# A hybrid decoder trunk in fp32: ScalarE of the mixer in written order, convolved tiles and gates finished in steps of slots, decay operands in other rooms

## The chip, the cores and the metric

The program runs on one NeuronCore of one Trainium2 chip, as one launch. The metric is the device time in microseconds (us). The kernel before took 2068.75, 2069.67 and 2070.12 us in three runs, so a median of 2069.67 us. Its profiled execution took 2069.44 us, of which 2067.7 us lie in the span of the profile. The names of the engines are TensorE (PE in the profile), VectorE (DVE), ScalarE (ACT), GpSimd (POOL) and SyncE (SP), which issues most of the transfers.

## The reference

Input and output are 512 positions of 1024 channels in fp32, and there are two layers. Cut to what matters here:

```python
# twice:
x = x + 0.5 * swiglu_1(rmsnorm(x))          # 1024 -> 2816 -> 1024
x = x + mixer(rmsnorm(x)) @ w_out
x = x + 0.5 * swiglu_2(rmsnorm(x))
# mixer: one projection of h, split into the inputs of three heads' groups
hg_q, hg_f, hg_i, hg_g, gd_q, gd_k, gd_v, gd_z, gd_b, gd_a, rg_x, rg_gate = split(h @ w_in)
# HGRN2, 4 heads of 64:   f = lb + (1-lb)*sigmoid(hg_f), k = 1-f, q = silu(hg_q)
#                         S_t = diag(f_t) S_{t-1} + k_t v_t^T,  o_t = S_t^T q_t
# gated delta, 4 of 128:  q, k, v = silu(conv4(...)), q and k normalised by head
#                         g = -exp(a_log)*softplus(gd_a + dt_bias), beta = sigmoid(gd_b)
#                         S_t = e^g_t (I - b_t k_t k_t^T) S_{t-1} + b_t k_t v_t^T
# RG-LRU, 256 channels:   xc = conv4(rg_x) + bias; r, i = sigmoid(block matmuls of xc)
#                         a = exp(-8 r softplus(-lam)); h_t = a_t h_{t-1} + sqrt(1-a_t^2) (i xc)_t
# each gated (silu(hg_g), silu(gd_z), gelu(rg_gate)), concatenated, projected by w_out
```

## The kernel before

Activations lie with channels on the 128 partitions and the 512 positions along the free axis. Every weight tile is split into two halves of fp32r: ScalarE casts it (`whi`, L229), VectorE forms the rest (`wlo`, L230). A product is then three matmuls: xh·whi (L268), xl·whi (L269) and xh·wlo (L270). One output tile of a projection (128 channels by 512 positions) is 8 steps of 3 matmuls. Its weights come as two tiles, of four steps each, and each tile needs one cast, one subtraction and one transfer.

The mixer of a layer issues 26 such projections in the order `MIX_ORDER` (k0 to k3 of the gated delta rule, then f and q of HGRN2, q0 to q3, v0 to v3, rx0, rx1, rg0, rg1, hg0, hg1, z0 to z3). `Slots.run` (L92) walks through them. One slot is two steps, 6 matmuls. After each slot every side line whose wait is over does its next piece; a line says with `yield (event, n)` that it wants n slots from an event, and with `yield n` that it wants n more slots. A projection's event is fired when its `then` (L575) has evicted the tile and issued the work behind it: the eviction by VectorE (times the row factor `rb`), for k, q, v and rx also the convolution (L588 or L590 on ScalarE and three L592 on VectorE), and silu, sigmoid or gelu on ScalarE.

In the mixer TensorE runs in the order in which the Python code issues its instructions: `manual_schedule(engines={PE})`, L610. The order of the other engines is set by a scheduler, which places their instructions by its own estimate of when each can start. All engines run their lists in order.

Three pieces of the mixer matter below. `gdn_gates` forms g (the `log1pexp` chain of small VectorE instructions, L501 to L519, L720) and from it eight tiles of 128 by 512 in fp32r (L730), the operands of eight decay matmuls (L747); ScalarE takes exp of three small matmuls (`gex`, L738) and of the decays (`DT`, L751). `gdn_k` transposes the silu'd keys (L760), sums their squares (L766), scales them (`Kn`, L795) and makes k·k (L786), whose result VectorE multiplies by DT (L787). `rglru` (the gate matmuls L1294, sigmoid L1296, Exp L1302, Tanh L1303, L1306 and L1307 on VectorE, Sqrt L1308, then L1310, the scan L1312 and L1313 on VectorE) stands beside the chunk chain of the gated delta rule (`chain`: L971, L979, L983, L995, L1007 on TensorE; L986, L989 and L1015 on ScalarE; L974, L1002 and L1011 on VectorE) and the HGRN2 products (`hgrn`: L1127, L1149, with copies L1140 and L1152 on ScalarE).

Of the kernel before, what the change touches and what calls it, by code (L numbers as in the profile page):

```python
# [6 lines left out]
F32R = mybir.dt.float32r  # L7
I32 = mybir.dt.int32
AF = mybir.ActivationFunctionType
# [4 lines left out]
P = 128  # L14
L = 2
D = 1024
S = 512
# [14 lines left out]
C_RCW = C_CW + 48  # L32
# [29 lines left out]
class Slots:  # L62
# [11 lines left out]
        event, n = w  # L74
        return event in self.at and self.now >= self.at[event] + n

    def add(self, line):
        self.sides.append([(None, 0), line])
        self.at.setdefault(None, 0)

    def step(self):

# [31 lines left out]
class Trunk:  # L114
# [452 lines left out]
    def project(self, then, event=None):  # L567

        ps = self.bank()
        w = self.weights()  # L570
        for k in range(KT):
            self.mm3_step(ps, w, self.X, k, KT, k)
            if k % 2 and k < KT - 1:
                yield
        then(ps)  # L575
        if event is not None:
            self.sl.fire(event)
        yield

    def conv(self, ps, w, bias=None):  # L580

        nc = self.nc
        pad = self.tmp((P, S + 4))
        nc.gpsimd.memset(pad[:, 0:4], 0.0)
        nc.vector.tensor_tensor(pad[:, 4:], ps, self.rb, ALU.mult)
        c = self.tmp()
        if bias is None:
            nc.scalar.activation(c, pad[:, 4:], AF.Copy, scale=w[3])  # L588
        else:
            nc.scalar.activation(c, pad[:, 4:], AF.Identity, scale=w[3], bias=bias)  # L590
        for i in range(3):
            nc.vector.scalar_tensor_tensor(c, pad[:, 1 + i:1 + i + S], w[i], c, ALU.mult, ALU.add)  # L592
        return c
# [13 lines left out]

    def mixer(self, l, nxt):
        nc = self.nc
        with self.tc.manual_schedule(engines={mybir.EngineType.PE}):  # L610
            self.mixer_in(l)
            self.mixer_out(l, nxt)

# [71 lines left out]
    def in_gd(self, l, m):  # L685

        c0 = l * NPC + C_CW + 4 * m

        def then(ps):
            if m == 0:  # L690
                self.Q = self.tile(self.mp, (P, 4, S), F32, "r_q")
            if m == 4:
                self.kt = self.spare(3)
            if m < 4:
                out = self.Q[:, m, :]
            elif m < 8:
                out = self.kt[:, m - 4, :]
            else:
                out = self.vt[m] = self.tmp()
            c = self.conv(ps, [self.par[:, c0 + i:c0 + i + 1] for i in range(4)])  # L700
            self.silu(out, c)

        self.vt = getattr(self, "vt", {})
        return self.project(then, f"gd{m}")

    def gdn_gates(self, l, ba):

        nc = self.nc
        sl = self.sl
        c0 = l * NPC  # L710
        v3 = lambda t: t.rearrange("p (c h) -> p c h", h=4)
        self.beta = self.tile(self.mp, (P, 16), F32, "beta")
        y = self.small(16, "g_y")
        dt = self.par[:, c0 + C_DT:c0 + C_DT + 4][:, None, :].to_broadcast([P, NJ, 4])
        nc.vector.tensor_tensor(v3(y), ba[:, :, 4:8], dt, ALU.add)
        sp = self.small(16, "g_sp")
        self.log1pexp(sp, y, 16)
        self.g = self.tile(self.mp, (P, 16), F32, "g")
        nea = self.nea[:, 4 * l:4 * l + 4][:, None, :].to_broadcast([P, NJ, 4])
        nc.vector.tensor_tensor(v3(self.g), v3(sp), nea, ALU.mult)  # L720
        gh = [self.small(16, f"g_{t}", F32R) for t in "hl"]
        nc.vector.tensor_copy(gh[0], self.g)
        nc.vector.tensor_tensor(gh[1], self.g, gh[0].bitcast(F32), ALU.subtract)

        low = self.tile(self.mp, (P, 4, S), F32R, "r_q")
        gm = []
        for c in range(NJ):
            gm.append([self.tile(self.mp, (P, 4, P), F32R, "gt", 4).rearrange("p a b -> p (a b)"), low[:, c, :]])
            for t, o in zip(gh, gm[c]):
                nc.vector.tensor_tensor(o.rearrange("p (a b) -> p a b", b=P),  # L730
                                        self.le[:, None, :].to_broadcast([P, 4, P]),
                                        bc(t[:, 4 * c:4 * c + 4].bitcast(F32), P), ALU.mult)
        yield 12
        ps = self.bank("mx", (P, 3, 16))
        for i, lhs in enumerate((self.le, self.gt, self.one)):
            nc.tensor.matmul(ps[:, i, :], lhsT=lhs, rhs=self.g, start=True, stop=True)
        self.ex = self.tile(self.mp, (P, 3, 16), F32, "gex")
        nc.scalar.activation(self.ex, ps, AF.Exp)  # L738
        self.nex = self.tile(self.mp, (P, 16), F32, "gnex")
        nc.vector.tensor_scalar(self.nex, self.ex[:, 0, :], -1.0, None, ALU.mult)  # L740

        self.DT = self.tile(self.mp, (P, 16, P), F32, "DT")
        pr = self.pair()
        pd = [pr[:, 0:1, :], pr[:, 1:2, :], self.bank("mx")[:, None, :], self.bank("mx")[:, None, :]]
        for c in range(NJ):
            for i in range(2):
                nc.tensor.matmul(pd[c][:, 0, :], lhsT=self.gt_r, rhs=gm[c][i], start=(i == 0), stop=(i == 1))  # L747
        for c, p in ((0, pr), (2, pd[2]), (3, pd[3])):
            n = p.shape[1]
            dt = self.DT[:, 4 * c:4 * (c + n), :]  # L750
            nc.scalar.activation(dt.rearrange("p a b -> p (a b)"), p.rearrange("p a b -> p (a b)"), AF.Exp)  # L751
            nc.vector.tensor_tensor(dt, dt, self.le[:, None, :].to_broadcast([P, 4 * n, P]), ALU.mult)
        nc.scalar.activation(v3(self.beta), ba[:, :, 0:4], AF.Sigmoid)
        sl.fire("DT")

    def gdn_tok(self, v):
# [272 lines left out]
    def in_z(self, l, h):  # L1029
        def then(ps):  # L1030

            z = self.Kn[:, 4 * h:4 * h + 4, :] if h < NJ - 1 else self.DT[:, 0:4, :]
            self.z[h] = z = z.rearrange("p a b -> p (a b)")
            self.nc.vector.tensor_tensor(z, ps, self.rb, ALU.mult)
            self.silu(z, z)

        self.z = getattr(self, "z", {})
        return self.project(then, f"z{h}")

    def gdn_out(self, l):  # L1040
        c0 = l * NPC
        yield ("o", 0)
        yield ("rg", 0)
        self.second((1, 2))
        yield 4
        for h in range(4):
            yield (f"z{h}", 3)
            ps = self.bank("mx", (P, 4, P))
            for c in range(NJ):
                self.nc.tensor.transpose(ps[:, c, :], self.Q[:, h, c * P:(c + 1) * P], self.ident)  # L1050
            self.out_parts(2 + h, ps.rearrange("p a b -> p (a b)"), self.z[h],
                           self.par[:, c0 + C_GDW:c0 + C_GDW + 1])


    def in_hf(self, l, i):
# [3 lines left out]
        def then(ps):  # L1059
# [13 lines left out]
            d["st"] = self.tile(self.mp, (P, NJ - 1, P), F32, f"hg_st{i}")  # L1073
            f, k = d["f"], d["k"]
            nc.vector.tensor_tensor(f, ps, self.rb, ALU.mult)
            nc.scalar.activation(f, f, AF.Sigmoid)
            o = 2 * l + i
            nc.vector.tensor_scalar(f, f, self.olb[:, o:o + 1], self.lb[:, o:o + 1], ALU.mult, ALU.add)
# [5 lines left out]
    def in_hq(self, l, i):  # L1084

        def then(ps):
            q = self.hg[i]["q"]
            self.nc.vector.tensor_tensor(q, ps, self.rb, ALU.mult)
            self.silu(q, q)

        return self.project(then, f"hq{i}")
# [110 lines left out]
                                sq.rearrange("p j (h v) -> p j h v", h=2), AX.X, ALU.add)  # L1202

    def hgrn(self, i, V):
        yield (f"hq{i}", 2 + i)
        if i == 1:
            self.hgo = self.tile(self.mp, (P, 16), F32, "hg_osq")
        for H in (0,) + LEVELS + (P,):
# [18 lines left out]
    def in_hg(self, l, i):  # L1227

        def then(ps):
            g = self.hgg[i] = self.hgqk[:, S:] if i == 0 else self.tile(self.mp, (P, S), F32, "hg1f")  # L1230
            self.nc.vector.tensor_tensor(g, ps, self.rb, ALU.mult)
            self.silu(g, g)

        self.hgg = getattr(self, "hgg", {})
        return self.project(then, f"hg_g{i}")

    def hgrn_out(self, l, V):
# [2 lines left out]
        yield ("hgv", 2)  # L1240
        yield ("merged", 0)
        for i in range(2):
            yield (f"hg_g{i}", 2)
            if i == 0:
                self.second((0,))
            pt = self.pair()[:, 0, :].rearrange("p (j t) -> p j t", t=P)
# [6 lines left out]
    def in_rx(self, l, i):  # L1253
        col = lambda c: self.par[:, l * NPC + c:l * NPC + c + 1]

        def then(ps):
            self.rx[i] = self.conv(ps, [col(C_RCW + 4 * i + j) for j in range(4)], col(C_RCB + i))

        self.rx = getattr(self, "rx", {})
        return self.project(then, f"rx{i}")  # L1260
# [1 line left out]
    def in_rg(self, l, i):  # L1262

        def then(ps):
# [4 lines left out]
                v = self.hgqk[:, 0:S]  # L1269
            self.rgl[i] = v  # L1270
            self.nc.vector.tensor_tensor(v, ps, self.rb, ALU.mult)
            self.nc.scalar.activation(v, v, AF.Gelu_apprx_tanh)

        self.rgl = getattr(self, "rgl", {})
# [2 lines left out]
    def rglru(self, l):  # L1277
# [5 lines left out]
        r, a = ra[:, 0:2, :], ra[:, 2:4, :]  # L1283
        bx = []
        for i in range(2):
            yield (f"rx{i}", GAP)
            xc = self.rx[i]
            if i == 0:
                igs = self.tile(self.mp, (P, 2, S), F32, "hg_sd")
# [14 lines left out]
        for i in range(2):  # L1304
            a2 = self.tmp()
            nc.vector.tensor_tensor(a2, a[:, i, :], a[:, i, :], ALU.mult)  # L1306
            nc.vector.scalar_tensor_tensor(r[:, i, :], a2, 1.0, r[:, i, :], ALU.add, ALU.mult)  # L1307
        nc.scalar.activation(r, r, AF.Sqrt)  # L1308
        for i in range(2):
            nc.vector.tensor_tensor(bx[i], bx[i], r[:, i, :], ALU.mult)  # L1310
# [81 lines left out]
KIND.update({26: ("rg", 0, None), 27: ("rg", 1, None)})  # L1392
KIND.update({20 + h: ("z", h, "states") for h in range(4)})

GAP = 4
SOLVE = 24


# [80 lines left out]
```

## Time and profile before

| | |
|---|---|
| Median of three runs | 2069.67 us |
| Profiled execution | 2069.44 us |
| Its span | 2067.7 us |
| TensorE busy | 2031.7 us, 98% |
| VectorE busy | 1097.7 us, 53% |
| ScalarE busy | 819.1 us, 40% |
| First mixer, roughly | 376 to 640 us of the span |
| Second mixer, roughly | 1399 to 1663 us of the span |

The profile shows one execution. Busy time is the time in which an engine works, and the rest of the span it waits or has nothing to do. In the rows of a timeline the first number is the start of the instruction from the start of the span, the second its duration, then engine, line, operation, written tile and read tiles, their sizes, and how many instructions are put together (x4); in brackets is the idle time of that engine just before and what ended it. Consecutive instructions overlap a little, so a duration is somewhat longer than the distance to the next start. The two mixers have the same program, so a wait in one has its twin in the other.

### The profile page before, as it was taken

The numbers are of one execution on the slowest core, as the hardware profiler recorded it, in microseconds if no ns is written. First come the engines' busy times: TensorE is split into PE (matmuls) and PEld (weight loads), VectorE is DVE, ScalarE is ACT, GpSimd is POOL, SyncE is SP. The second block draws the span as 40 slices with busy tenths as digits, with TensorE's granted clock in tenths as the row PEclk, the third lists the DMA queues.
The fourth block names the chain that finished last, engine by engine and source line by source line (L and its number), as shares of the span: only waits on it lengthen the run. The fifth ranks groups of instructions, "written<-read, shape, count | busy, mean of one in ns | idle before, by whom it ended". The sixth has DMA issues, their size and how long they took to land.

```text
span 2067.7 us, 29619 instructions
## 1 busy us (share of the span) xinstructions
PE 2031.7 (98%) x11808; PEld 1653.4 (80%) x11808; DVE 1097.7 (53%) x2037; ACT 819.1 (40%) x1546; POOL 10.5 (1%) x41
## 2 busy tenths in 40 slices
PE   9999999989999999999999999998999999999998
PEld 7888888867888888888888888887778888888887
DVE  6434435767675443434644344466766754444345
ACT  5323223565664332323433232246557533223233
POOL 0000000000000000000000000000000000000000
PEclk9999999999999999999999999999999999999999
DMA  5232222222122232232222322222221222222222
GB/s 188 92 100 94 92 98 81 88 77 66 53 72 92 92 102 92 92 99 89 97 92 92 99 95 92 94 76 87 81 54 62 82 92 92 97 97 92 94 90 72
DMA packets 69115, 185.43 MB, mean 90 GB/s; under 512 B 20976, under 2 KB 22768, under 8 KB 68976
## 3 DMA queue, kind: packets, MB, share of 16 engines
q1 hardware_dynamic: 67712, 181.99, 26.8%
q8 instruction: 92, 1.51, 0.3%
q10 hardware_dynamic: 1120, 1.42, 0.2%
q14 instruction: 47, 0.39, 0.1%
q0 software_dynamic: 144, 0.13, 0.0%
HBM read 180.10 MB, written 2.62 MB: 88 GB/s over the span
## 4 chain that ended last, share of the span: by engine, by line
PE 92%; DVE 4%; ACT 2%; DMA 1%; issue 1%; SPq 0%; DVEq 0%; ACTq 0%
PE mm L268 17%; PE mm L270 17%; PE mm L269 17%; PE mx L268 12%; PE mx L270 12%; PE mx L269 12%; DVE tmp L592 1%; DVE wlo L230 1%; DMA gt<-dl 0%; PE mx L786 0%; PE mx L760 0%; PE mx L1007 0%; PE mx L983 0%; PE mx L829 0%; PE hx L1294 0%
## 5 line engine op out<-in xcount | busy, mean ns | idle before, releaser
L229 ACT CAST whi<-wraw 128x512 fp32r<-128x512 f32 (+2 forms) x688 | 416.1, 607 | 956.2 <-PE mm L269 472.3
L230 DVE TENSOR_TENSOR wlo<-wraw,whi 128x512 fp32r<-128x512 f32 (+2 forms) x688 | 460.0, 670 | 342.7 <-ACT whi L229 334.6
L268 PE MATMUL mm<-xh,whi 128*128 128x512 f32 x1120 | 454.8, 406 | 0.7 <-ACT whi L229 0.7
L270 PE MATMUL mm<-xh,wlo 128*128 128x512 f32 x1120 | 442.1, 395 | 0.1
L269 PE MATMUL mm<-xl,whi 128*128 128x512 f32 x1120 | 440.9, 394 | 0.2 <-DVE xl L337 0.2
L268 PE MATMUL mx<-xh,whi 128*128 128x512 f32 x704 | 278.2, 395 | 0.0
L270 PE MATMUL mx<-xh,wlo 128*128 128x512 f32 x704 | 277.2, 394 | 0.0
L269 PE MATMUL mx<-xl,whi 128*128 128x512 f32 x704 | 276.1, 392 | 0.0
L270 PEld LDWEIGHTS mm<-xh,wlo 128*128 128x128 f32 x1120 | 211.0, 188 | 50.5 <-DVE wlo L230 0.5
L268 PEld LDWEIGHTS mm<-xh,whi 128*128 128x128 f32 x1120 | 211.0, 188 | 47.1 <-ACT whi L229 1.1
L269 PEld LDWEIGHTS mm<-xl,whi 128*128 128x128 f32 x1120 | 211.7, 189 | 46.0 <-issue 1.0
L268 PE MATMUL mm<-y,whi 128*128 128x512 f32 x468 | 185.2, 396 | 0.3 <-ACT y L291 0.3
L270 PE MATMUL mm<-y,wlo 128*128 128x512 f32 x468 | 184.3, 394 | 0.0
L269 PE MATMUL mm<-y,whi 128*128 128x512 f32 x468 | 184.0, 393 | 0.2 <-DVE y L292 0.2
L270 PEld LDWEIGHTS mx<-xh,wlo 128*128 128x128 f32 x704 | 132.2, 188 | 31.5
L269 PEld LDWEIGHTS mx<-xl,whi 128*128 128x128 f32 x704 | 132.5, 188 | 30.5
L268 PEld LDWEIGHTS mx<-xh,whi 128*128 128x128 f32 x704 | 132.2, 188 | 29.7 <-ACT whi L229 0.2
L402 DVE TENSOR_TENSOR fu<-mx,rb 128x512 f32<-128x512 f32 x88 | 60.9, 692 | 140.0 <-PE mx L270 140.0
L268 PE MATMUL mx<-y,whi 128*128 128x512 f32 x340 | 134.4, 395 | 0.0
L270 PE MATMUL mx<-y,wlo 128*128 128x512 f32 x340 | 133.9, 394 | 0.0
L269 PE MATMUL mx<-y,whi 128*128 128x512 f32 x340 | 133.4, 392 | 0.0
L396 DVE TENSOR_TENSOR fg<-mm,rb 128x512 f32<-128x512 f32 x88 | 60.8, 691 | 134.7 <-PE mm L270 134.1
(354 smaller groups left out, 1995.3 us busy)
## 6 DMA issues: line engine op xcount, KB each, us to landing
wraw<-in_wgu SPq DMA_DIRECT2D x174, 512.0 KB, 3.6
wraw<-in_wd SPq DMA_DIRECT2D x64, 512.0 KB, 3.5
wraw<-in_win SPq DMA_DIRECT2D x52, 512.0 KB, 3.5
wraw<-in_wd SPq DMA_DIRECT2D x32, 384.0 KB, 3.0
wraw<-in_wout SPq DMA_DIRECT2D x16, 512.0 KB, 3.2
wraw<-in_wv SPq DMA_DIRECT2D x8, 264.0 KB, 2.5
x<-in_x SPq DMA_DIRECT2D x3, 512.0 KB, 6.1
wraw<-in_wgu SPq DMA_DIRECT2D x3, 256.0 KB, 6.2
```

The source lines that it names most:

```text
L229: self.nc.scalar.copy(hi, raw)
L230: self.nc.vector.tensor_tensor(lo, raw, hi.bitcast(F32), ALU.subtract)
L268: nc.tensor.matmul(ps, lhsT=a, rhs=xh, start=(n == 0), stop=False)
L269: nc.tensor.matmul(ps, lhsT=a, rhs=xl, start=False, stop=False)
L270: nc.tensor.matmul(ps, lhsT=b, rhs=xh, start=False, stop=(n == size - 1))
L396: nc.vector.tensor_tensor(g, pg, rb, ALU.mult)
L402: nc.vector.tensor_tensor(u, pu, rb, ALU.mult)
L592: nc.vector.scalar_tensor_tensor(c, pad[:, 1 + i:1 + i + S], w[i], c, ALU.mult, ALU.add)
```

## The change

The change has four parts.

- `manual_schedule` now names ScalarE as well: in the mixer ScalarE runs in the order in which the code issues its instructions.
- `project` no longer issues all the work behind a projection at once. `then` is a generator; its first piece (the eviction) comes with the last slot, and a side line `finish` does the rest in later slots: the conv's ScalarE instruction one slot after the eviction, silu two slots after that, sigmoid, silu and gelu of f, q, g, gates and z one slot after the eviction. The event is fired by that line when it ends. GAP goes from 4 to 1 and other waits by one or two, so that the lines behind an event start in the slot of before, and `rglru` waits 2 slots after rx0 and rx1 where it waited 4. It also waits 2 slots before Sqrt.
- Beta's sigmoid (L753 before, L725 after) is written ahead of the `log1pexp` chain. It stood last in `gdn_gates`.
- The eight decay operands are in the tiles `gd_v` and `r_q`, the later rooms of values and queries. Four of them were in the ring `gt`.

```diff
-        then(ps)
-        if event is not None:
-            self.sl.fire(event)
+        rest = then(ps)
+        def finish(n):
+            while n is not None:
+                yield n
+                n = next(rest, None)
+            if event is not None:
+                self.sl.fire(event)
+        line = finish(next(rest))
+        self.sl.add(line, next(line))
         yield
...
+        yield 1
         c = self.tmp()
...
-        with self.tc.manual_schedule(engines={mybir.EngineType.PE}):
+        with self.tc.manual_schedule(engines={mybir.EngineType.PE, mybir.EngineType.Activation}):
...
-            c = self.conv(ps, [self.par[:, c0 + i:c0 + i + 1] for i in range(4)])
+            c = yield from self.conv(ps, [self.par[:, c0 + i:c0 + i + 1] for i in range(4)])
+            yield 2
             self.silu(out, c)
...
+        nc.scalar.activation(v3(self.beta), ba[:, :, 0:4], AF.Sigmoid)
...
-        low = self.tile(self.mp, (P, 4, S), F32R, "r_q")
+        parts = [self.tile(self.mp, (P, 4, S), F32R, t) for t in ("gd_v", "r_q")]
-            gm.append([self.tile(self.mp, (P, 4, P), F32R, "gt", 4).rearrange("p a b -> p (a b)"), low[:, c, :]])
+            gm.append([t[:, c, :] for t in parts])
...
-            yield (f"rx{i}", GAP)
+            yield (f"rx{i}", 2)
...
+        yield 2
         nc.scalar.activation(r, r, AF.Sqrt)
...
-GAP = 4
+GAP = 1
```

TensorE's order is that of before but for the names of the decay operands and for the two gate matmuls L1294 of rx0 and of rx1, which stand one slot earlier in each mixer. On SyncE one weight load of each mixer stands later, behind the transfers of DT and T. ScalarE has 30 loads of activation tables where it had 42 (14 for 20 in each mixer). VectorE's list has the same work, and its order is still the scheduler's.

On VectorE around the decay operands, before: `g_h` and `g_l` are the two halves of g, the last two rows of the first piece belong to the conv of k1 and k2. The weights of k3 (`wlo_3207`) stand 19 rows ahead of the first L730.

```order
L515 TENSOR_SCALAR sp_r_3078<-sp_r_3078 128x16
L230 TENSOR_TENSOR wlo_3207<-wraw_3150,whi_3206 128x512
L514 TENSOR_TENSOR sp_r_3078<-sp_r_3078,sp_w_3076 128x16
...
L723 TENSOR_TENSOR g_l_3101<-g_3098,g_h_3100 128x16
L730 TENSOR_TENSOR gt_3105<-cst_134,g_h_3100 128x512
L730 TENSOR_TENSOR r_q_3104<-cst_134,g_l_3101 128x512
...
L592 SCALAR_TENSOR_TENSOR tmp_3187<-tmp_3184,par_76,tmp_3187 128x512
L585 TENSOR_TENSOR tmp_3238<-mm_3203,rb_3036 128x512
```

The same place now (L743 is L730 of before, L232 is L230, L603 is L592, L595 is L585; `wlo_3199` and `wlo_3203` are the two halves of k3's weights, `tmp_3212` is the conv of k1):

```order
L736 TENSOR_TENSOR g_l_3102<-g_3099,g_h_3101 128x16
L743 TENSOR_TENSOR gd_v_3105<-cst_134,g_h_3101 128x512
L743 TENSOR_TENSOR r_q_3106<-cst_134,g_l_3102 128x512
...
L232 TENSOR_TENSOR wlo_3199<-wraw_3142,whi_3198 128x512
L232 TENSOR_TENSOR wlo_3203<-wraw_3142,whi_3202 128x512
L603 SCALAR_TENSOR_TENSOR tmp_3212<-tmp_3182,par_76,tmp_3212 128x512
L595 TENSOR_TENSOR tmp_3236<-mm_3195,rb_3036 128x512
L603 SCALAR_TENSOR_TENSOR tmp_3212<-tmp_3182,par_76,tmp_3212 128x512 x2
```

The weights of k3 moved from ahead of the eight decay operands to behind them, and the three steps of k1's conv behind those.

On ScalarE at the decay exponentials, before (`gex` is L738, the three `DT` are L751, `y_603_3139<-tmp_3187` is the silu of k1, `y_603_3139<-tmp_3241` that of k2):

```order
L738 ACT_TABLE_LOAD
L738 ACTIVATE gex_3268<-mx_3264 128x48
L596 ACT_TABLE_LOAD
L596 ACTIVATE y_603_3139<-tmp_3187 128x512
L766 ACTIVATE gt_3198,ksq_3119<-mx_3193 128x128 x4
L751 ACT_TABLE_LOAD
L751 ACTIVATE DT_3272<-hx_3273 128x1024
L596 ACT_TABLE_LOAD
L596 ACTIVATE y_603_3139<-tmp_3241 128x512
L751 ACT_TABLE_LOAD
L751 ACTIVATE DT_3272<-mx_3274 128x512
```

And now (L607 is L596, L751 is L738, L764 is L751, L599 is L588):

```order
L599 ACTIVATE tmp_3212<-tmp_3182,par_76 128x512
L607 ACTIVATE y_600_3137<-tmp_3212 128x512
L231 CAST whi_3242<-wraw_3196 128x512
L231 CAST whi_3246<-wraw_3196 128x512
L751 ACT_TABLE_LOAD
L751 ACTIVATE gex_3260<-mx_3256 128x48
L764 ACTIVATE DT_3264<-hx_3265 128x1024
L764 ACTIVATE DT_3264<-mx_3266 128x512
L764 ACTIVATE DT_3264<-mx_3267 128x512
L599 ACTIVATE tmp_3282<-tmp_3236,par_76 128x512
```

The silu of k1 and two casts moved ahead of gex; the three exponentials of DT stand together, and the silu of k2 is behind them.

On VectorE at the RG-LRU scan, before (`wlo_5363` and `wlo_5367` are the two halves of z0's weights, `hg_sd_5116` and `y_834_4855` belong to the RG-LRU):

```order
L1307 SCALAR_TENSOR_TENSOR y_834_4855<-tmp_5274,y_834_4855 128x512
L1307 SCALAR_TENSOR_TENSOR y_834_4855<-tmp_5277,y_834_4855 128x512
L1310 TENSOR_TENSOR hg_sd_5116<-hg_sd_5116,y_834_4855 128x512 x2
L1312 SCALAR_TENSOR_TENSOR y_834_4855<-y_834_4855,hg_sd_5116 128x512 x2
L1313 TENSOR_TENSOR hg_sd_5116<-y_834_4855,hg_f_5174 128x512
L1313 TENSOR_TENSOR hg_sd_5116<-y_834_4855,hg_qk_5254 128x512
L1231 TENSOR_TENSOR hg_qk_5254<-mm_5287,rb_3036 128x512
L1002 SCALAR_TENSOR_TENSOR state_5343<-state_5226,gex_3268,mx_5338 128x128 x4
L1011 TENSOR_TENSOR r_q_3896<-mx_5348,r_q_3896 128x4x128
L230 TENSOR_TENSOR wlo_5363<-wraw_5288,whi_5362 128x512
L230 TENSOR_TENSOR wlo_5367<-wraw_5288,whi_5366 128x512
```

And now (L1324 is L1307, L1328, L1330 and L1331 are L1310, L1312 and L1313, L1246 is L1231, L1014 is L1002, L1023 is L1011, L986 is L974; `wlo_5359` is the first half of z0's weights):

```order
L1246 TENSOR_TENSOR hg_qk_5251<-mm_5268,rb_3036 128x512
L1014 SCALAR_TENSOR_TENSOR state_5332<-state_5223,gex_3260,mx_5327 128x128 x3
...
L1324 SCALAR_TENSOR_TENSOR y_830_4846<-tmp_5311,y_830_4846 128x512
L1014 SCALAR_TENSOR_TENSOR state_5332<-state_5223,gex_3260,mx_5327 128x128
L1023 TENSOR_TENSOR r_q_3893<-mx_5337,r_q_3893 128x4x128
L986 SCALAR_TENSOR_TENSOR gt_5380<-mx_5379,gnex_3262,gd_v_4780 128x128 x4
L1328 TENSOR_TENSOR hg_sd_5081<-hg_sd_5081,y_830_4846 128x512 x2
L1330 SCALAR_TENSOR_TENSOR y_830_4846<-y_830_4846,hg_sd_5081 128x512 x2
L1331 TENSOR_TENSOR hg_sd_5081<-y_830_4846,hg_f_5178 128x512
L1331 TENSOR_TENSOR hg_sd_5081<-y_830_4846,hg_qk_5251 128x512
L232 TENSOR_TENSOR wlo_5359<-wraw_5269,whi_5358 128x512
```

The RG-LRU's tail moved by one chunk of the chain: it stood ahead of the eviction of hg0 and of chunk 2's state update, and stands behind chunk 2's update and chunk 3's L974. On ScalarE Exp and Tanh stand together now, behind chunk 2's L986 and L989, with that chunk's four L1015 between Tanh and Sqrt; before, Exp stood ahead of chunk 1's L1015, Tanh behind it, and Sqrt ahead of chunk 2's L986.

## Rows read from the trace of the kernel before

**Rows 1.** The page: busy time by engine, and one costly group (busy, mean ns).

```profile
PE 2031.7 (98%) x11808; PEld 1653.4 (80%) x11808; DVE 1097.7 (53%) x2037; ACT 819.1 (40%) x1546; POOL 10.5 (1%) x41
...
L229 ACT CAST whi<-wraw 128x512 fp32r<-128x512 f32 (+2 forms) x688 | 416.1, 607 | 956.2 <-PE mm L269 472.3
```

**Rows 2.** TensorE's waits: line, waited for, us in total, times, longest.

```profile
PE mx L786 <- ACT DT L751: 14.1, 2, 7.0
PE mx L747 <- ACT gex L738: 2.1, 2, 1.1
PE hx L1149 <- ACT gt L766: 1.5, 2, 0.8
```

**Rows 3.** TensorE's timeline at the decay matmuls.

```profile
407.29 0.39 PE L270 MATMUL mm<-xh,wlo 128*128 128x512 f32 x1
...
411.50 0.50 PE L747 MATMUL mx<-gt,cst_r 128*128 128x512 f32 x1 [1.06 <-ACT gex L738]
...
420.66 2.08 PE L786 MATMUL mx<-y 128*128 128x128 f32 x8 [7.04 <-ACT DT L751]
```

**Rows 4.** VectorE's timeline at the decay operands: first L730, and the row behind the eighth.

```profile
402.94 0.68 DVE L730 TENSOR_TENSOR gt<-cst,g_h 128x512 fp32r<-128x512 f32 x1
...
407.76 0.74 DVE L592 SCALAR_TENSOR_TENSOR tmp<-tmp,par,tmp 128x512 f32<-128x512 f32 x1
```

**Rows 5.** ScalarE's timeline at the decay exponentials.

```profile
409.94 1.28 ACT L738 ACT_TABLE_LOAD   x1
411.24 0.21 ACT L738 ACTIVATE gex<-mx 128x48 f32<-128x48 f32 x1
...
412.76 0.63 ACT L596 ACTIVATE y<-tmp 128x512 f32<-128x512 f32 x1
...
415.73 1.02 ACT L751 ACTIVATE DT<-hx 128x1024 f32<-128x1024 f32 x1
```

**Rows 6.** Stretches around the wait for DT: length, busy time by engine, granted clock.

```profile
413.00:420.00 7.00, 0.62 (x3) 0.18 (x1) 2.53 (x4) 6.92 (x14) 0.10 (x1) 0.85 0.21 75
...
422.00:424.00 2.00, 2.00 (x8) 1.71 (x8) 1.29 (x2) 0.38 (x1) 0.00 (x0) 0.50 0.00 0
```

**Rows 7.** ScalarE's timeline at the transposes of q0 and of q3.

```profile
469.42 1.63 ACT L1140 COPY gd_v<-hg_sc 32x256 f32<-32x256 f32 x4
...
474.29 0.73 ACT L588 ACTIVATE tmp<-tmp,par 128x512 f32<-128x512 f32 x1 [0.29 <-DVE tmp L585]
...
506.53 0.60 ACT L1200 ACTIVATE gd_v<-hx 128x512 f32<-128x512 f32 x1
```

**Rows 8.** TensorE's timeline at the transposes of q0 and of q3.

```profile
473.36 0.60 PE L760 MATMUL mx<-cst_r,r_q 128*128 128x128 f32 x4
...
506.59 0.60 PE L760 MATMUL mx<-cst_r,r_q 128*128 128x128 f32 x4
```

**Rows 9.** TensorE's timeline from chunk 2's L983 to the third matmul of z0.

```profile
576.33 1.06 PE L983 MATMUL mx<-gt,y 128*128 128x128 f32 x8
...
590.97 0.40 PE L270 MATMUL mm<-xh,wlo 128*128 128x512 f32 x1
```

**Rows 10.** ScalarE's timeline at the RG-LRU.

```profile
569.78 1.06 ACT L1302 ACTIVATE y<-y 128x1024 f32<-128x1024 f32 x1
...
571.91 1.04 ACT L1303 ACTIVATE y<-y 128x1024 f32<-128x1024 f32 x1
...
575.69 1.28 ACT L1308 ACT_TABLE_LOAD   x1
...
577.95 1.13 ACT L986 ACTIVATE gt<-mx,bk 128x128 f32<-128x128 f32 x4
```

**Rows 11.** VectorE's timeline at the RG-LRU.

```profile
578.08 1.29 DVE L1310 TENSOR_TENSOR hg_sd<-hg_sd,y 128x512 f32<-128x512 f32 x2 [2.59 <-ACT y L1308]
579.29 2.33 DVE L1312 TENSOR_TENSOR_SCAN y<-y,hg_sd 128x512 f32<-128x512 f32 x2
581.54 0.67 DVE L1313 TENSOR_TENSOR hg_sd<-y,hg_f 128x512 f32<-128x512 f32 x1
```

More of the change, by code (lines that the diff above doesn't have):

```diff
@@ L75, in due, with add @@
         return event in self.at and self.now >= self.at[event] + n
-    def add(self, line):
-        self.sides.append([(None, 0), line])
-        self.at.setdefault(None, 0)
+    def add(self, line, n=0):
+        key = id(line)
+        self.sides.append([(key, n), line])
+        self.at[key] = self.now
     def step(self):
@@ L752, in gdn_gates @@
             nc.vector.tensor_tensor(dt, dt, self.le[:, None, :].to_broadcast([P, 4 * n, P]), ALU.mult)
-        nc.scalar.activation(v3(self.beta), ba[:, :, 0:4], AF.Sigmoid)
         sl.fire("DT")
@@ L1034, in then @@
             self.nc.vector.tensor_tensor(z, ps, self.rb, ALU.mult)
+            yield 1
             self.silu(z, z)
@@ L1046, in gdn_out @@
         for h in range(4):
-            yield (f"z{h}", 3)
+            yield (f"z{h}", 2)
             ps = self.bank("mx", (P, 4, P))
@@ L1075, in then @@
             nc.vector.tensor_tensor(f, ps, self.rb, ALU.mult)
+            yield 1
             nc.scalar.activation(f, f, AF.Sigmoid)
@@ L1088, in then @@
             self.nc.vector.tensor_tensor(q, ps, self.rb, ALU.mult)
+            yield 1
             self.silu(q, q)
@@ L1204, in hgrn @@
     def hgrn(self, i, V):
-        yield (f"hq{i}", 2 + i)
+        yield (f"hq{i}", 1 + i)
         if i == 1:
@@ L1231, in then @@
             self.nc.vector.tensor_tensor(g, ps, self.rb, ALU.mult)
+            yield 1
             self.silu(g, g)
@@ L1242, in hgrn_out @@
         for i in range(2):
-            yield (f"hg_g{i}", 2)
+            yield (f"hg_g{i}", 1)
             if i == 0:
@@ L1256, in then @@
         def then(ps):
-            self.rx[i] = self.conv(ps, [col(C_RCW + 4 * i + j) for j in range(4)], col(C_RCB + i))
+            self.rx[i] = yield from self.conv(ps, [col(C_RCW + 4 * i + j) for j in range(4)], col(C_RCB + i))
         self.rx = getattr(self, "rx", {})
@@ L1271, in then @@
             self.nc.vector.tensor_tensor(v, ps, self.rb, ALU.mult)
+            yield 1
             self.nc.scalar.activation(v, v, AF.Gelu_apprx_tanh)
```

## The prediction

> **What bounds the kernel now.** I read the page first, then TensorE's waits, then the timelines around each. TensorE works 2031.7 of 2067.7 us [rows 1], so 36 us are to be had at most; ScalarE at 40% bounds nothing by its sum. Of the waits the reader is to see one line that stands out: L786 waits for DT, 7.0 us, once in each mixer, 14.1 us in all [rows 2]. The next, L747 for gex, is 1.1 us each. In the timeline the wait ends at 420.66 [rows 3]. ScalarE, not the data, set it: between gex at 411.24 and DT stand the silu of k1, other tables and squares, and the first DT comes at 415.73 [rows 5]. The wait has a second price. The granted clock was 0.85 in the stretch that holds it and 0.50 when the matmuls ran again, from 422 to 424 [rows 6]; that is the lower of the two levels. Eight matmuls of L786 took 2.08 us there [rows 3] where eight of the same size take 1.06 at full clock (L983) [rows 9]. From the twelve projection matmuls, L786 and the transposes up to the return of the clock I estimate 1.75 us lost in each mixer.
>
> **The change, part by part.** All sums are for the first mixer, in the time of the profiled execution (2069.44 us, 0.23 below the median of the runs; I let that go). The second has the same program and the same waits, "2" in the column of times [rows 2], so it counts double.
>
> *Stretch A, k0 to the first HGRN2 product.* The three DT now follow gex at once. But two things that stood ahead now stand behind on VectorE, and it runs its list in order. The small chain that forms g has both halves of k2's weights, k0's eviction and k0's conv in it; by its steps I get the first L730 about 1 us later than 402.94, at 403.9. Eight of them take 4.82 (402.94 to 407.76) [rows 4], to 408.7; only then comes k3's first wlo, 0.68 like an L730, so TensorE's third matmul of k3 starts at 409.6 where it started at 407.29 [rows 3]: a new wait of 2.3 us. Next on VectorE are k3's other wlo, 0.6, then k1's three L592 with k2's eviction among them, 0.74 each [rows 4] and 0.6: they end at 412.6. On ScalarE the silu of k1 waits for that (0.63), then two casts (0.54 to 0.6 each by the mean of 607 ns [rows 1]), a table load of 1.28, and gex, 0.21 [rows 5]: 412.6 + 0.7 + 1.1 + 1.3 + 0.2 = 415.9. L747's fourth pair, which needs the bank that gex frees, would start at 412.6 after the first wait and starts at 415.95: a second new wait, 3.35 us, where 1.06 stood. DT is then 1.02 + 0.54 behind gex, at 417.5; TensorE comes to L786 at 418.0, as it has the last pair and six matmuls before it. So the wait for DT goes, and L786 starts 2.65 us earlier than at 420.66. I let the clock stay full here: +1.75 gained. k3's silu is late for its transpose by 1.1 us (its L592 stand behind a product with DT and two wlo, its silu behind squares, conv and casts). A gains 2.65 + 1.75 - 1.1 = 3.3. Bounds: if both new waits stay away, 7.04 + 1.06 + 1.75 - 1.1 = 8.75 gained; if the clock falls all the same, 1.55.
>
> *Stretch B, HGRN2 products beside q.* Copies, convs and silus of ScalarE stand in the order of the code. Worked out at two places. The L588 of q0 stands behind the four L1140 (469.42, 1.63 [rows 7]), so it ends 0.73 later, at 471.8; three L592 of 0.74 follow, then the silu, 0.63: 474.6 against 473.36 for the transpose [rows 8], a wait of 1.3. Silu of q3 stands behind L1200, which ends about 507.1 [rows 7]: + 0.6 makes 507.7 against 506.59 [rows 8], a wait of 1.05. Four smaller ones (two L1127, L1149, the transpose of q2) come by the same way to 3.7, an estimate. Against the sum of 6.05 stand about 3.35 of before's own waits in this stretch (L1149's 0.8 [rows 2] and its like): B loses 2.7. Bounds: 3.35 gained, if ScalarE is always in time, and 6.05 lost, if the old waits come on top.
>
> *Stretch C, RG-LRU and the gates.* Before, TensorE practically doesn't wait here, so there is nothing to win. The end of chunk 2's L983 is 577.4 and the third matmul of z0 starts at 590.97 [rows 9]: 13.6 us. That matmul needs the first wlo of z0, which now stands on VectorE behind the whole tail of the RG-LRU, and Exp stands on ScalarE behind chunk 2's L986 and L989, which wait for that L983. The chain: about 0.1 to the first L986, L986 and L989 2.1 (1.13 for four, 1.0 to the next [rows 10]), table load 1.28, Exp and Tanh 2.0 [rows 10], the two L1307 1.3 by the form of L1310, L1002 and L1011 0.9, four L1015 1.25 (by L986), table load 1.28, Sqrt 1.06 by the form of Exp, two L1310 1.2 [rows 11], scan 2.25 (579.29 to 581.54), two L1313 1.2, wlo 0.68: 16.6, and some 0.4 at the hand-overs between engines make 17.0. So z0's third matmul waits 3.4 us. In before the same chain started at 569.78 [rows 10] and was over when wlo was due. Smaller: the gate matmuls L1294, a slot earlier while the convs of rx0 and rx1 end no sooner, wait 0.9 together; the transpose of v2 0.35; chunk 3's and the output's waits 0.8. C loses 5.45. Bounds: 0 (all hidden) and 8.
>
> *Without a price.* The other rooms of the decay operands cost VectorE the same eight writes; HGRN2's clearing of `gd_v` now waits for the decay matmuls, but VectorE is there no sooner. Beta is needed far behind. The weight load that moved on SyncE comes for a tile needed slots later. ScalarE loads 12 tables fewer, 12 x 1.28 = 15.4 us [rows 5], off TensorE's path except where the chains above hold a load.
>
> Sum: 2 x (-3.3 + 2.7 + 5.45) = +9.7; 2069.4 + 9.7 = 2079.
>
> **Rivals.**
> - *Faster: behind A the written order costs nothing.* VectorE waits 2.59 us for Sqrt in before [rows 11]; if such slack swallows B and C and A gains what I count, 2 x -3.3 = -6.6, 2062.8; if A opens in full, -17.5, 2052. It decides whether z0's wlo ends before 590.97, so whether the chain takes under 13.6 us. For it: ScalarE is 40% busy and loses 15 us of loads. Against it: each step of the chain has its row. The Trainium skill speaks for it ("ScalarE: Activation LUTs", What ACT_TABLE_LOAD costs): besides about 1.28 us of load it counts a drain of about 1.38, by which 12 loads fewer free 32 us of ScalarE and not 15. The row shows the load at 409.94 for 1.28 and gex at 411.24 [rows 5], so no such drain behind it, and by the page my chain in C would be longer, too.
> - *No change.* A and B as counted, but z0's wlo in time: 2 x (-3.3 + 2.7 + 2.05) = +2.9, 2072. Then the DT wait has only moved. For it: my 3.4 is the difference of two sums of some 15 us, each hand-over of which I took from other places. Against: an error of 3.4 in 17 is much.
> - *Slower still: the clock falls in the new waits.* If the granted clock goes to 0.50 behind the waits of 2.3 and 3.35 us in A, and behind z0's 3.4, each mixer loses 1.75 at A again and about as much at z0: +9.7 + 7 = 2086. For it: the clock did fall behind 7.04 us [rows 6]. Against: nothing of 2 to 4 us stands in this trace with a clock beside it, and A's waits have matmuls between them. The Trainium skill ("TensorE: Matmul & The Clock Gate", What's actually happening) has the rate halved when the array has been idle and given back when it has been busy for a while; the rows agree, and by the rule this rival is open, not excluded.
>
> **How the numbers follow.** My forecast (a loss of about 6 to 14 us) has 38%, the clock rival 16%, no change 23%, faster 23%. A measurement of this kernel tells 0.2% from no change, 4.1 us, so "same" is 2065.5 to 2073.8. Faster 23%, same 22%, slower 55% (a few of the forecast's cases are near the bound). The likeliest's own range is 2075 to 2083; the range for 8 in 10 takes in the no-change case, the nearer half of the faster one and the clock: 2060 to 2088.
>
> **What would show it.** In A: L786 no longer among the long waits; k3's L270 waiting for wlo about 2.3 us, L747 for gex about 3.4; L730 of before's line starting near 404; granted clock 1.0 behind them. In B: the transposes of q0 and q3 waiting for silus about 1 us. In C: z0's first L270 waiting for wlo about 3.4 us, with the scan directly ahead of it on VectorE, and Exp starting after chunk 2's L989. I am wrong if z0's third matmul doesn't wait, if gex comes near 411 again, or if TensorE's idle time falls below 36 us.

## The result and the profile after

The changed kernel takes 2090.83 us in the median of four runs (2085.22 to 2090.96) against 2069.89 us, the kernel before's median of four: 1.0095 times as long, 95% interval 1.0078 to 1.0113. The forecast was 2079 us with 2060 to 2088 as its range: right in direction, outside the range in size. The page of the changed kernel, its span and engines, answering to [rows 1]:

```profile
span 2089.0 us, 29529 instructions
PE 2044.3 (98%) x11808; PEld 1659.6 (79%) x11808; DVE 1098.5 (53%) x2037; ACT 793.8 (38%) x1534; POOL 10.5 (1%) x41
```

The span grew by 21.3 us. TensorE's idle time grew by 8.7 of them (44.7 for 36.0), its busy time by 12.6 with the same 11808 matmuls. So more than half of the loss isn't in waits at all. (The prediction's "36 us are to be had at most" leaves this out: a matmul at half rate counts as busy for its whole length.) TensorE's waits of the changed kernel, answering to [rows 2] (L272 is L270 of before, L760 is L747, L772 is L760, L1164 is L1149, L1311 is L1294, L909 is L897):

```profile
PE mm L272 <- DVE wlo L232: 10.7, 4, 3.4
PE mx L760 <- ACT gex L751: 4.5, 2, 3.3
PE mx L772 <- ACT r_q L607: 4.1, 4, 1.1
PE mx L772 <- ACT tmp L607: 2.8, 4, 0.9
PE hx L1164 <- ACT hg1f L1177: 2.2, 2, 1.1
PE mx L772 <- ACT y L607: 1.8, 2, 0.9
PE hx L1311 <- DVE tmp L603: 1.8, 4, 0.6
PE mx L909 <- issue: 1.8, 1, 1.8
```

The wait for DT is gone from the list, and in its place stand those that the forecast named. Stretch A of the first mixer, TensorE, then VectorE, then ScalarE, answering to [rows 3 to 5]:

```profile
409.24 0.51 PE L272 MATMUL mm<-xh,wlo 128*128 128x512 f32 x1 [2.03 <-DVE wlo L232]
...
410.06 0.63 PE L272 MATMUL mm<-xh,wlo 128*128 128x512 f32 x1
...
415.77 0.80 PE L760 MATMUL mx<-gd_v,cst_r 128*128 128x512 f32 x1 [1.24 <-ACT gex L751]
...
419.35 1.50 PE L798 MATMUL mx<-y 128*128 128x128 f32 x8
```
```profile
403.69 0.68 DVE L743 TENSOR_TENSOR gd_v<-cst,g_h 128x512 fp32r<-128x512 f32 x1
...
408.51 1.28 DVE L232 TENSOR_TENSOR wlo<-wraw,whi 128x512 fp32r<-128x512 f32 x2
409.71 0.74 DVE L603 SCALAR_TENSOR_TENSOR tmp<-tmp,par,tmp 128x512 f32<-128x512 f32 x1
```
```profile
412.54 0.63 ACT L607 ACTIVATE y<-tmp 128x512 f32<-128x512 f32 x1 [8.47 <-DVE tmp L603]
413.07 1.12 ACT L231 CAST whi<-wraw 128x512 fp32r<-128x512 f32 x2
414.21 1.28 ACT L751 ACT_TABLE_LOAD   x1
415.51 0.21 ACT L751 ACTIVATE gex<-mx 128x48 f32<-128x48 f32 x1
```

k3's weights stand behind the eighth operand, gex behind k1's silu, two casts and a table, all within half a us of the times worked out. But the matmul at 410.06 takes 0.63 where one takes 0.39 at full clock: TensorE fell to half rate 0.8 us after the wait of 2.03 had ended. The gex wait is only 1.24 there, for the matmuls ahead of it took longer; in the second mixer, where they ran at full clock, it is 3.26:

```profile
1451.36 0.80 PE L760 MATMUL mx<-gd_v,cst_r 128*128 128x512 f32 x1 [3.26 <-ACT gex L751]
```

L798, the L786 of before, starts at 419.35 and not at the 418.0 of the forecast, since the eight matmuls ahead of it ran at half rate. Stretches of the changed kernel's span (length, busy time by engine, granted clock), answering to [rows 6]; the first at full rate, then the six that have half rate in them:

```profile
406.00:410.00 4.00, 1.97 (x9) 1.32 (x8) 4.00 (x8) 0.00 (x0) 0.00 (x0) 1.00 0.00 0
410.00:421.00 11.00, 9.76 (x32) 7.68 (x32) 7.69 (x13) 6.45 (x12) 0.10 (x1) 0.53 0.29 96
491.00:496.00 5.00, 4.37 (x44) 3.40 (x43) 1.19 (x4) 1.51 (x4) 0.00 (x0) 0.66 0.01 3
601.00:605.00 4.00, 4.00 (x16) 3.36 (x16) 1.53 (x3) 3.72 (x12) 0.00 (x0) 0.57 0.39 131
1451.00:1455.00 4.00, 3.64 (x11) 2.92 (x12) 2.79 (x5) 3.59 (x9) 0.00 (x0) 0.57 0.39 131
1526.00:1530.00 4.00, 3.75 (x26) 2.71 (x25) 1.81 (x5) 1.66 (x9) 0.00 (x0) 0.57 0.02 4
1632.00:1639.00 7.00, 6.11 (x19) 5.15 (x20) 3.38 (x6) 4.25 (x12) 0.00 (x0) 0.51 0.22 75
```

TensorE's busy time in each, times what the clock lacks to 1.00 (9.76 x 0.47, 4.37 x 0.34, ...), gives 4.6 + 1.5 + 1.7 + 1.6 + 1.6 + 3.0 = 14.0 us. The same for the kernel before, from its two stretches:

```profile
417.00:425.00 8.00, 4.34 (x15) 3.77 (x16) 3.60 (x5) 5.33 (x9) 0.00 (x0) 0.57 0.10 32
1441.00:1449.00 8.00, 4.56 (x16) 3.90 (x17) 3.38 (x5) 5.12 (x9) 0.00 (x0) 0.57 0.13 42
```

is 3.8; taken tightly around the half rate (4.09 and 4.31 us of busy time at 0.50) it is 4.2. So some 10 of the 21.3 us are half rate, and the rest is waits with what hangs on them. The two aren't quite separate: some 2 us of the half rate at 410 passed in time that TensorE would otherwise have waited for gex. Stretch C of the first mixer, the same three engines, answering to [rows 9 to 11]:

```profile
600.04 0.50 PE L272 MATMUL mm<-xh,wlo 128*128 128x512 f32 x1 [3.32 <-DVE wlo L232]
```
```profile
594.65 1.29 DVE L1328 TENSOR_TENSOR hg_sd<-hg_sd,y 128x512 f32<-128x512 f32 x2 [2.25 <-ACT y L1326]
595.86 2.33 DVE L1330 TENSOR_TENSOR_SCAN y<-y,hg_sd 128x512 f32<-128x512 f32 x2
...
599.30 1.28 DVE L232 TENSOR_TENSOR wlo<-wraw,whi 128x512 fp32r<-128x512 f32 x2
```
```profile
585.19 1.28 ACT L1319 ACT_TABLE_LOAD   x1
586.49 1.06 ACT L1319 ACTIVATE y<-y 128x1024 f32<-128x1024 f32 x1
...
593.56 1.06 ACT L1326 ACTIVATE y<-y 128x1024 f32<-128x1024 f32 x1
```

The chain from Exp over Sqrt and the scan to z0's wlo is there link by link, and z0's third matmul waits 3.32 us for it (forecast 3.4). In the second mixer the matmul behind the same wait is at half rate from its start:

```profile
1632.89 0.80 PE L272 MATMUL mm<-xh,wlo 128*128 128x512 f32 x1 [3.36 <-DVE wlo L232]
```

### The profile page after: what moved, and what is told of

Its sections match the earlier page's. It is cut to its first block, busy times and chain, and to the rows that moved or that the text cites. A ratio compares the mean times of both kernels' runs of the same rounds, so it can differ in the third digit from the quotient of the medians.

```text
span 2089.0 us, 29529 instructions
## 1 busy us (share of the span) xinstructions
PE 2044.3 (98%) x11808; PEld 1659.6 (79%) x11808; DVE 1098.5 (53%) x2037; ACT 793.8 (38%) x1534; POOL 10.5 (1%) x41
## 4 chain that ended last, share of the span: by engine, by line
PE 89%; DVE 6%; ACT 3%; issue 1%; DMA 0%; SPq 0%; DVEq 0%; ACTq 0%
PE mm L270 16%; PE mm L272 16%; PE mm L271 16%; PE mx L270 12%; PE mx L272 12%; PE mx L271 11%; DVE tmp L603 2%; DVE wlo L232 1%; ACT whi L231 1%; PE mx L772 1%; PE hx L1142 1%; PE hx L1311 0%; PE mx L798 0%; PE mx L841 0%; DVE tmp L595 0%
## 5 line engine op out<-in xcount | busy, mean ns | idle before, releaser
L231 ACT CAST whi<-wraw 128x512 fp32r<-128x512 f32 (+2 forms) x688 | 410.2, 607 | 837.9 <-PE mx L271 436.9
L232 DVE TENSOR_TENSOR wlo<-wraw,whi 128x512 fp32r<-128x512 f32 (+2 forms) x688 | 455.0, 669 | 352.3 <-ACT whi L231 347.4
L270 PE MATMUL mm<-xh,whi 128*128 128x512 f32 x1120 | 457.1, 408 | 0.0
L272 PE MATMUL mm<-xh,wlo 128*128 128x512 f32 x1120 | 445.1, 397 | 10.7 <-DVE wlo L232 10.7
L270 PE MATMUL mx<-xh,whi 128*128 128x512 f32 x704 | 278.2, 395 | 0.0
L272 PE MATMUL mx<-xh,wlo 128*128 128x512 f32 x704 | 277.2, 394 | 0.0
L272 PEld LDWEIGHTS mm<-xh,wlo 128*128 128x128 f32 x1120 | 212.3, 190 | 63.1 <-DVE wlo L232 12.9
L270 PEld LDWEIGHTS mm<-xh,whi 128*128 128x128 f32 x1120 | 212.3, 190 | 46.4 <-issue 1.0
L270 PE MATMUL mm<-y,whi 128*128 128x512 f32 x468 | 185.1, 396 | 0.0
L272 PE MATMUL mm<-y,wlo 128*128 128x512 f32 x468 | 184.3, 394 | 0.0
L272 PEld LDWEIGHTS mx<-xh,wlo 128*128 128x128 f32 x704 | 132.2, 188 | 31.6
L270 PEld LDWEIGHTS mx<-xh,whi 128*128 128x128 f32 x704 | 132.3, 188 | 29.6
L270 PE MATMUL mx<-y,whi 128*128 128x512 f32 x340 | 134.4, 395 | 0.0
L272 PE MATMUL mx<-y,wlo 128*128 128x512 f32 x340 | 133.9, 394 | 0.0
```

The lines of the kernel that those rows point to most:

```text
L231: self.nc.scalar.copy(hi, raw)
L232: self.nc.vector.tensor_tensor(lo, raw, hi.bitcast(F32), ALU.subtract)
L270: nc.tensor.matmul(ps, lhsT=a, rhs=xh, start=(n == 0), stop=False)
L272: nc.tensor.matmul(ps, lhsT=b, rhs=xh, start=False, stop=(n == size - 1))
```

## The experiments

My theory was that the written order of ScalarE makes VectorE reach two weights late, and that the half rate behind those waits costs as much as the waits. The rivals were that the steps of slots cost the time, and that the clock is a small part of it.

**The parts of the change, one by one.** `undo_act` takes the written order back alone:

```diff
-        with self.tc.manual_schedule(engines={mybir.EngineType.PE, mybir.EngineType.Activation}):
+        with self.tc.manual_schedule(engines={mybir.EngineType.PE}):
```

> The changed kernel with ScalarE left to the scheduler again in the mixer; steps of slots, beta and the rooms of the decay operands stay. Theory (the written order of ScalarE is what makes VectorE reach two weights late, and half-rate stretches of TensorE follow those waits): k3's wlo and z0's wlo stand ahead of the decay operands and the RG-LRU tail again, so both waits of about 2 and 3.3 us per mixer go, with their half-rate stretches; the three DT stay together, so the wait for DT is some 3 us in place of 7. Time 2056 to 2066 us. Rival 1 (the steps of slots and later conv pieces cost the time, whoever orders ScalarE): 2080 or more. Rival 2 (the other parts do nothing): 2069 to 2071, with the 7 us wait for DT.

Measured: 2054.92 us, ratio to the kernel before 0.9931 (0.9919 to 0.9944), a little below what was expected. Its first two waits:

```profile
PE mx L798 <- ACT DT L764: 5.3, 2, 2.6
PE mx L760 <- ACT gex L751: 2.1, 2, 1.1
```

No wlo is late any more, and of the half rate one stretch is left in the two mixers (417.4 to 420.8). In a kernel that has the other three parts the written order costs 36 us (34 by the two ratios); everything else in the change gains 14 to 15. The written order without the steps of slots was not tried. `steps` is the kernel before with the slot steps alone (`project`, `conv`, the shorter waits; beta and the rooms as before):

> The kernel before with the steps of slots alone: convolved tiles, gates and f are finished in later slots, ScalarE stays with the scheduler, beta and the rooms of the decay operands as before. Theory (the steps are the part that gains: with them the scheduler puts the three DT together, ahead of the silu of k2): the wait for DT falls from 7.0 to some 2.6 us per mixer, with less half rate behind it: 2053 to 2058 us, as with all but the written order. Rival (beta's place or the rooms make the gain): 2066 to 2071.

Measured: 2057.77 us, 0.9942 (0.9930 to 0.9955), as the theory had it. `b_both` is the kernel before with the other two parts:

```diff
+        nc.scalar.activation(v3(self.beta), ba[:, :, 0:4], AF.Sigmoid)   # ahead of log1pexp
-        nc.scalar.activation(v3(self.beta), ba[:, :, 0:4], AF.Sigmoid)   # behind DT
-            gm.append([self.tile(self.mp, (P, 4, P), F32R, "gt", 4).rearrange("p a b -> p (a b)"), low[:, c, :]])
+            gm.append([t[:, c, :] for t in parts])                       # rooms gd_v and r_q
```

> The kernel before with beta's sigmoid ahead of the chain of g and the decay operands in gd_v and r_q, nothing else. Theory (these two parts are worth nothing by themselves; the silu of k2 still stands between the first DT and the other two): wait for DT 7 us, 2068 to 2071 us. Rival (they free the decay stretch): 2055 to 2062.

Measured: 2068.57 us, 0.9992 (0.9983 to 1.0001): no difference that can be told. The wait for DT of `b_both`, then of `steps`:

```profile
PE mx L786 <- ACT DT L752: 12.0, 2, 6.0
```
```profile
PE mx L798 <- ACT DT L763: 7.4, 2, 3.7
```

So the gain inside the change is the steps of slots: the silu of k2 reaches the scheduler later, and the three DT come together. The wait of 3.7 us that is left is longer than the 2.6 expected.

**z0's wait.** `sqrt3` moves Sqrt one slot back, so that z0's casts and its wlo stand ahead of the RG-LRU's tail:

```diff
-        yield 2
+        yield 3
         nc.scalar.activation(r, r, AF.Sqrt)
```

> The changed kernel with 3 slots instead of 2 ahead of Sqrt, so that the casts of z0's weights stand ahead of Sqrt on ScalarE and z0's wlo ahead of the tail of the RG-LRU on VectorE. Theory (z0's wait of 3.3 us per mixer comes from that order, and TensorE runs at half rate after it): 6.6 us of waits and some 4 to 5 us of half rate go, 2079 to 2081 us. Rival (the scan is on the path to the end, the wait only moves to the RG-LRU's output): 2088 to 2091.

Measured: 2088.99 us, 1.0095 (1.0081 to 1.0109): the rival's time. Three rows of it, of VectorE, ScalarE and TensorE:

```profile
599.24 0.74 DVE L616 SCALAR_TENSOR_TENSOR tmp<-hx,par,hg_qk 128x512 f32<-128x512 f32 x1
```
```profile
600.02 0.62 ACT L293 CAST y<-tmp 128x512 fp32r<-128x512 f32 x1 [3.81 <-DVE tmp L616]
600.54 1.14 ACT L998 ACTIVATE gt<-mx,bk 128x128 f32<-128x128 f32 x4
```
```profile
600.96 1.44 PE L1019 MATMUL mx<-gt,DT 128*128 128x128 f32 x5 [3.33 <-ACT gt L998]
```

z0's wlo is in time, but hg0's product L616 still stands behind the tail on VectorE, ScalarE's cast L293 waits for it, and L998, written behind that cast, can't pass it. The wait moved to chunk 3's L1019 and kept its 3.3 us. What both kernels share is the tail standing late. `rg2` writes it earlier:

```diff
-        yield ("rg1", 0)
         nc.scalar.activation(a, r, AF.Exp)
...
         nc.scalar.activation(r, r, AF.Sqrt)
         for i in range(2):
...
             nc.vector.tensor_tensor_scan(h, a[:, i, :], bx[i], 0.0, ALU.mult, ALU.add)
-            nc.vector.tensor_tensor(bx[i], h, self.rgl[i], ALU.mult)
+        yield ("rg1", 0)
+        for i in range(2):
+            nc.vector.tensor_tensor(bx[i], r[:, i, :], self.rgl[i], ALU.mult)
```

> The changed kernel, ScalarE in written order, with the RG-LRU written earlier: Exp and Tanh straight behind the gates' sigmoids, Sqrt two slots later, product and scan behind it, and only the product with the gelu waits for rg1. Theory (z0's wait of 3.3 us per mixer, and the wait of as much for chunk 3's operand that took its place when only Sqrt was moved, are both VectorE's tail of the RG-LRU of some 5 us standing too late; written ahead of chunk 2's work it harms neither): both waits go, with the half rate behind them, 6.6 us and 3 to 5 us: 2079 to 2083 us. Rival (the tail is in somebody's way wherever it stands in a written order): 2087 to 2091.

Measured: 2077.97 us, 1.0036 (1.0023 to 1.0048): 12.9 us less than the changed kernel and a us below what was expected; neither wait is in its list. In its profile TensorE's idle time is 5.5 us less than the changed kernel's (6.7 of z0 gone, 2.0 more for gex) and its busy time, with the same matmuls, 6.4 less.

**k3's wait.** `dec9` issues the decay operands 9 slots later (`yield 9` ahead of `parts`, `yield 3` for `yield 12`):

> The changed kernel with the eight decay operands issued 9 slots later, so that VectorE makes k3's weights after the first two of them and k1's conv among them. Theory: the wait for k3's wlo (2.0 us per mixer) goes, the wait for gex stays at some 2 to 3 us since the silu of k1 still stands ahead of it; L786 starts some 3 us earlier, the half-rate stretch of 10 us in the first mixer shortens or goes: 2078 to 2085 us. Rival (ScalarE's order ahead of gex sets it alone): L786 starts as late as now, 2089 to 2092.

Measured: 2078.95 us, 1.0051 (1.0038 to 1.0063), as the theory had it. Its first and third wait:

```profile
PE mm L272 <- DVE wlo L232: 6.7, 2, 3.4
...
PE mx L761 <- ACT gex L752: 3.0, 2, 1.5
```

Of the four late weights two are left, z0's; the gex wait fell to 1.5, further than expected.

**The clock by itself.** `fill_z0` and `fill_all` put matmuls into the waits:

```diff
         ps = self.bank()
         w = self.weights()
+        for _ in range({"z0": 13, "gd7": 8}.get(event, 0)):    # fill_z0: z0's 13 alone
+            self.nc.tensor.matmul(ps, lhsT=self.gt_r, rhs=self.X[0][0], start=True, stop=True)
```

(`fill_all` has 13 more ahead of L747's last pair, in a bank of their own.)

> The changed kernel with 13 matmuls of 128x512 more in each mixer, ahead of z0's projection, written into its bank and overwritten by it: they stand in the 3.3 us in which TensorE waits for z0's wlo. The computation is the same otherwise. Theory (TensorE drops to half rate some us after that wait because it idled): with the wait filled the stretch of half rate behind it goes, so the kernel with 26 matmuls more is faster, by 3 to 5 us, 2086 to 2088 us. Rival (the half rate there has another cause, or the clock is not what the time is lost by): no change, 2090 to 2092, or slower by up to 6 us where the wait isn't where the matmuls are.

Measured: 2087.25 us, 1.0087 (1.0073 to 1.0101), 3.6 us less with 26 matmuls more. The time alone doesn't settle it, for one run in four of the changed kernel took 2085.22. The clock does: over z0's place in the two mixers, where the changed kernel fell to half rate (601 and 1632), it now stays full:

```profile
600.00:606.00 6.00, 5.72 (x32) 4.58 (x31) 4.53 (x9) 3.99 (x12) 0.00 (x0) 1.00 0.28 87
1630.00:1640.00 10.00, 9.67 (x48) 7.83 (x47) 8.53 (x13) 6.30 (x21) 0.00 (x0) 1.00 0.16 53
```

> The changed kernel with 34 more matmuls of 128x512 in each mixer, whose results nothing reads, in three of its waits: 8 ahead of k3's projection, 13 ahead of L747's last pair, 13 ahead of z0's projection. The computation is the same otherwise. Theory (of the 21 us lost, some 10 are half-rate stretches that follow these waits; filled, TensorE stays at full clock there and only the stretch behind the solve, some 1.7 us per mixer, is left): 2080 to 2084 us, 7 to 11 us less than the changed kernel in spite of 68 matmuls more, and granted clock 1.00 from 400 to 480 and from 590 to 610. Rival (the waits themselves are the loss, the clock a small part): 2089 to 2093.

Measured: 2076.17 us, 1.0028 (1.0017 to 1.0039): 14.7 us less with 68 matmuls more, better than expected. Stretches of `fill_all` over the places of half rate:

```profile
406.00:412.00 6.00, 5.84 (x28) 4.56 (x28) 5.96 (x11) 0.00 (x0) 0.00 (x0) 1.00 0.15 48
412.00:417.00 5.00, 4.78 (x21) 3.54 (x20) 2.47 (x5) 4.28 (x7) 0.10 (x1) 1.00 0.29 94
...
600.00:610.00 10.00, 9.59 (x43) 7.50 (x42) 9.34 (x25) 5.18 (x12) 0.00 (x0) 1.00 0.47 159
```

The waits for wlo and gex are filled, not mended: 15.2 us of them became 1.2 and 68 matmuls. No stretch of the two mixers is at half rate, and the gain is near the 14.0 us worked out above. It isn't the clock alone: the stretch behind the solve, which I had left in, went too, and the waits ahead of it (L909, 1.8 us in the first mixer, L1183, 1.1 us in the second, both "issue") aren't in this run's list. What makes them come and go stays open.

**Together.** `written` has `dec9` and `rg2` under the written order, `written_k1` also puts k1's silu behind the DT (`yield 5 if m == 5 else 2`).

> ScalarE in written order as in the changed kernel, with both repairs: decay operands 9 slots later and the RG-LRU written earlier. Theory (the two losses have separate causes and add): 2078.95 + 2077.97 - 2090.83 = 2066 us, 2064 to 2069, so level with the kernel before; gex's wait of 1.5 us, the late transposes of q and k and a half-rate stretch behind the solve are left. Rival (they share the loss): 2074 to 2078.

Measured: 2069.97 us, 0.9997 (0.9988 to 1.0005), a us over what was expected and, in us, halfway between the sum of the two repairs (2066) and the rival (2074). The ratios, each to the kernel before run beside it, decide for the sum: 1.0051 + 1.0036 - 1.0095 = 0.9992 lies in the interval, 2074 us (1.0017) doesn't.

> As the run with both repairs in written order, and the silu of k1 three slots later, so that gex and the three DT stand ahead of it on ScalarE. Theory (gex waits for that silu): the wait of 1.5 us per mixer for gex falls by 0.6 to 1.2 us, 2062 to 2066 us. Rival (gex waits for the decay operands or the casts anyway): as without it, 2064 to 2069.

Measured: 2066.71 us, 0.9983 (0.9974 to 0.9992), and gex is no longer among the larger waits. The time lies in the rival's range, 0.7 us above the theory's; what speaks for the theory is the list and the 3.3 us less than `written`. `undo_dec9` is `undo_act` with `dec9`'s edit:

> All but the written order of ScalarE (2054.9 us), and the eight decay operands issued 9 slots later, which lets the scheduler make k1's conv among them and put the silu of k1 ahead of gex, so that DT follows gex without another table. Theory (what is left of the wait for DT, 2.65 us per mixer, is that silu and its tables between gex and DT): the wait goes, gex's stays at 1 to 2 us: 2048 to 2052 us. Rival (the wait moves to gex or to the decay operands themselves, by as much): 2054 to 2057.

Measured: 2046.63 us, 0.9887 (0.9872 to 0.9903), the fastest and 1.4 us below what was expected. It beats the kernel before by 23 us and the changed one by 44. Its two largest waits:

```profile
PE mx L773 <- ACT y L607: 2.1, 4, 0.8
PE hx L1165 <- DVE hg_st L1191: 1.5, 2, 0.8
```

The waits for DT and for gex are gone, and no stretch of its two mixers is at half rate. `undo_dec9_rg2` adds `rg2`:

> The fastest so far (steps of slots, beta, rooms, decay operands 9 slots later, ScalarE left to the scheduler; 2046.6 us) with the RG-LRU written earlier. Theory (with ScalarE left to the scheduler no wait stands at the RG-LRU, so its place is worth nothing): 2045 to 2049 us. Rival (the earlier tail pushes into the chunk chain): 2050 to 2056.

Measured: 2049.45 us, 0.9898 (0.9883 to 0.9913), just outside: 2.8 us more than without it (2.3 by the ratios, whose intervals overlap). An early tail gains nothing where nothing had to be mended, and may cost something.

## Why the prediction was wrong

- *Stretch A, the waits:* right. k3 2.03 us (2.3 forecast), gex 3.26 in the mixer at full clock (3.35), k3's transpose 0.9 (1.1). In the two mixers TensorE's idle time of A is 6.2 us less than before (forecast 3.1 less; 2.0 of the difference is gex's shorter wait in the first mixer).
- *Stretch B:* right in kind. q0's transpose waits 1.07 (1.3), q3's 0.97 (1.05). Idle time 4.5 us more (5.4).
- *Stretch C:* right. z0 3.32 and 3.36 (3.4), the gate matmuls 0.9 per mixer (0.9). Idle time 11.7 us more (10.9).
- *The step that failed* is "I let the clock stay full here: +1.75 gained". The forecast had 3.5 us given back in two mixers and nothing lost at z0 or behind the solve. Measured: 14.0 us lost at half rate where the kernel before lost about 4, so some +10 where -3.5 stood: about 6 of the 14 in A, 3 in B, 5 in C. Without half rate (`fill_all`) the time is 2076 us, 3 below the forecast. The rival with the falling clock had the mechanism, with 16%; its 2086 was too low because a stretch of half rate lasted longer than the one I had priced it by (9.8 us of busy time from 410 to 421), and because I looked at three waits and not at the one behind the solve.
- The Trainium skill ("TensorE: Matmul & The Clock Gate", What's actually happening) has the rate halved when the array has been idle. The trace agrees in kind: 1.00 up to 410, 0.53 from 410 to 421, behind a wait of 2.03 us.
- That the table loads saved on ScalarE (12 of 1.28 us) would be worth nothing off TensorE's path fits the runs: the kernel with 12 loads fewer is the slower one, and `undo_act`, faster by 36 us, has 6 of them back. Between gex and DT they were on the path. In the order of before four loads stand between gex and the last DT; with none there (`undo_dec9`) the wait for DT is gone.

## What to carry to other kernels

Price a wait of TensorE as the wait and the half rate behind it, and look in the trace of before for the shortest wait that has a fall behind it. Below that, keep both cases in the range: the same wait of 2.0 us had a fall behind it in one mixer here and none in the other. An order fixed for one engine also fixes who is late on the engines that it hands work to, so undo the order alone before judging the rest of a change: here the rest was worth 14 to 15 us. A wait that is mended by moving one instruction may only change its place; ask what then stands behind the long piece.

## What was not expected of the hardware

The fall of the clock has no fixed place at a wait: in the first mixer the matmuls behind z0's wait ran at full rate from 600.04 to 601.1, and the half rate came then; in the second the clock fell at 1632.0, 0.9 us before the same wait had ended. The same wait of 2.0 us for k3's weights was followed by half rate at 410 in the first mixer and by none in the second, where the fall came at 1451.1, at the end of gex's 3.26. One run in four of the changed kernel took 2085.22 us at a mean clock of 0.993, the others 2090.8 to 2091.0 at 0.990 or 0.991, so part of this cost differs from run to run of the same program.
